# Where and on which engine the gate part of layer 2's modulation vector is computed

## The chip, the core and the metric

The kernel runs on one core of one Trainium2 chip. The core has five engines, each with its own in-order queue of instructions: TensorE (PE in the profile: matmuls, with PEld for the loading of the stationary operand), VectorE (DVE), ScalarE (ACT), GpSimd (POOL) and SyncE (SP, which here only issues DMA transfers). The engines wait for one another with semaphores. The metric is the device time of one execution in microseconds (us); lower is better.

## The reference

Two layers are applied to 256 latent tokens x (sample A, s = 0) and 256 context tokens (sample B, s = 1), each 2048 wide. Both layers start from a modulation vector that depends on a conditioning vector alone, one for the latent tokens and one for the context:

```
def adaln_params(cond, w_mod, b_mod):
    return jnp.split(jax.nn.silu(cond) @ w_mod + b_mod, 3, axis=-1)   # shift, scale, gate

def modulate(x, gain, shift, scale):
    return rmsnorm(x, gain) * (1 + scale) + shift

def deltanet_layer(x, ctx, c, c_ctx, ..., update_ctx):               # layer 2
    sh, sc, gt = adaln_params(c, w_mod, b_mod)
    sh_c, sc_c, gt_c = adaln_params(c_ctx, w_mod, b_mod)
    ...
    x = x + gt[:, None] * deltanet_out(o_xf + flip_t(o_xb), zx, o_norm, w_out)
    if update_ctx:                                                   # not in the last layer
        ctx = ctx + gt_c * deltanet_out(o_cf + flip_t(o_cb), zc, o_norm, w_out)
```

`w_mod` is 2048 x 6144 in float32. Shift and scale of layer 2 are used for both samples, at the start of the layer. Its gate is used for sample A alone, and only at the layer's very end. Layer 1 has neighbourhood attention (8 heads, "NA"), latent attention (8 heads, "MLA") and an output product; layer 2 is a gated DeltaNet; a final norm follows.

## The kernel before

Every dense product is made in float32 precision out of three products of halves: a weight block is loaded as `raw` (four buffers, DMA at L71), its high part `whi` is taken by ScalarE (L77) and the rest `wlo` by VectorE (L78), and TensorE makes hi by hi (L90), hi by lo (L91) and lo by hi (L92). One `unit` is a 128-column block of outputs for all 512 tokens: two weight halves of 8 x 3 matmuls each. A scheduler puts the instructions of each engine in order from the program's order, the buffers and an estimate of its own of when each is ready; the queue of each engine then runs in that order. A transfer waits in SP's queue for its buffer, and all that stand behind it wait too.

The modulation vector of a layer, `mods[l]`, has 48 blocks of 128, made in 12 chunks of 512 columns: chunks 0 to 3 are the shift, 4 to 7 the scale, 8 to 11 the gate. A chunk needs the 2048 x 512 float32 block of `w_mod`, which comes in eight transfers of 512 KB into `mraw`. There are two ways to make a chunk:

- `adaln` (L107), on TensorE: the conditioning is the stationary operand (32 columns wide, four row groups side by side), the weights are streamed through into the PSUM tile `pmod` (L127). VectorE copies it to `macc` (L133), TensorE transposes it (L136, `pmt`), and VectorE adds up the row groups and the bias (L138, L139). Both samples cost no more than one.
- `adaln_lanes` (L147), on VectorE: for each of 16 slices of 128 weight rows and each sample, one instruction adds slice times conditioning to `lacc` (L161 for the first slice, L163 for the others): 32 instructions on 128x512 elements for a chunk. They are called lane steps below. Then TensorE adds up the partitions with a matmul against ones (L170, `pml`), and VectorE adds the bias (L173). `lacc` and `pml` have one buffer each.

Both are generators. `later` (L307) strings them together, and each weight half of a `unit` (L316) advances the one in `ahead` by `pace` steps, so that the pieces lie between the pieces of other work in the program's order.

The program goes through layer 1 in these stages, with the chunks of layer 2 that each of them holds:

- the NA heads (seven of them one after another, each with its units of q, k, v and gate). `ahead` holds layer 1's own chunks 8 to 11 and layer 2's chunks 0 and 1, all as lane steps, with `pace` 1;
- units and rope for MLA, then the eighth NA head. From here `ahead` holds chunks 2, 3 and 8 of layer 2 as `adaln`, in a pool `mr2`, with three buffers for `mraw`;
- the eight MLA heads (L348, L381, L372 to L388 are attention's instructions), one step of `ahead` each; after them chunk 9 as `adaln` (L473), and the split of the gated heads into `gh`, `gl` (L480, L481);
- the output product: 16 units with the weights `ab_wo`, each followed by `x1A` and `x1B` (L493). Here chunks 4 to 7 stand as lane steps, begun after the first of these units;
- the modulate of layer 2 (L221 to L229, into `hh` and `hl`), while the first two units of layer 2 already consume it block by block. Chunks 10 and 11 stand here as `adaln` (L499, L504);
- then layer 2 (its first units are U_BA, whose output ScalarE takes at L635 and L636, and the K unit).

The gate of layer 2 is read by `project` (L606 to L611) near the end of the kernel, at `mods[1][:, 32 + u, 0:1]`: sample 0 only.

Of the kernel before, what the change touches and what calls it, by code (L numbers as in the profile page):

```python
# [8 lines left out]
F32 = mybir.dt.float32  # L9
F32R = mybir.dt.float32r  # L10
AF = mybir.ActivationFunctionType
ALU = mybir.AluOpType
# [14 lines left out]
def trunk_kernel(ctx: ExitStack, tc: tile.TileContext, g):  # L27
    nc = tc.nc
    V, A, PE, P = nc.vector, nc.scalar, nc.tensor, nc.gpsimd
# [14 lines left out]
    def cst(name, shape, src=None):  # L44
        t = const.tile(shape, F32, name=name, tag=name)
        if src is not None:
            nc.scalar.dma_start(t, src)
        return t
# [16 lines left out]
    mods = [cst(f"mod{l}", [128, 48, 2]) for l in range(2)]  # L65
# [80 lines left out]

    def adaln_lanes(l, ps, pm, tp, chunks, after=None):  # L147

        wm, bmod, gain = ((g["ab_wm"], ab_bmod, ab_gain), (g["dn_wm"], dn_bmod, dn_gain))[l]
        for ch in chunks:  # L150
            acc = tp.tile([128, 2, 512], F32, name="lacc", tag="lacc", bufs=1)
            for kg in range(4):
                for i in range(2):
                    raw = tp.tile([128, 2, 512], F32, name="mraw", tag="mraw", bufs=3)
                    with tc.issue_after(after) if after else nullcontext():
                        nc.sync.dma_start(raw, wm[ch, kg].rearrange("p (q c) -> p q c", q=4)[:, 2 * i:2 * i + 2])
                    for q in range(2):
                        k = 4 * kg + 2 * i + q
                        for s in range(2):
                            if k == 0:  # L160
                                V.tensor_scalar(acc[:, s], raw[:, q], cond[:, k, s:s + 1], None, op0=ALU.mult)  # L161
                            else:
                                V.scalar_tensor_tensor(acc[:, s], raw[:, q], cond[:, k, s:s + 1], acc[:, s],  # L163
                                                       op0=ALU.mult, op1=ALU.add)
                    if i == 0 or kg < 3:
                        yield
            pt = ps.tile([128, 4, 2], F32, name="pml", tag=pm, bufs=1)
            for j in range(4):
                for s in range(2):
                    PE.matmul(pt[:, j, s:s + 1], acc[:, s, j * 128:j * 128 + 128], ones[:, 0:1], start=True, stop=True)  # L170
            f = slice(4 * ch, 4 * ch + 4)
            md = mods[l][:, f]
            V.tensor_tensor(md, pt, bmod[:, f].unsqueeze(2).broadcast_to([128, 4, 2]), op=ALU.add)  # L173
            if 4 <= ch < 8:
                f = slice(4 * ch - 16, 4 * ch - 12)
                V.tensor_scalar(Am[l][:, f], md, 1.0, None, op0=ALU.add)
                V.tensor_tensor(Am[l][:, f], Am[l][:, f], gain[:, f].unsqueeze(2).broadcast_to([128, 4, 2]), op=ALU.mult)
            yield

    def steps(it, n=1000):  # L180
        for _ in range(n):
            if next(it, it) is it:
                break
# [18 lines left out]
    def blocks_of(*tiles, n=T):  # L202
        return [[t[:, c:c + 128] for t in tiles] for c in range(0, n, 128)]
# [39 lines left out]
    with tc.tile_pool(name="s0", bufs=2) as tp, tc.tile_pool(name="s0p", bufs=1, space=PSUM) as ps:  # L243
# [26 lines left out]
        def mods_of(j):  # L270
            k0, n = GROUPS[j]
            return adaln(0, ps, ("pmod", "aux"), tp, [(k0, n), (16 + k0, n)], bufs=MB)
# [8 lines left out]
        for j, (k0, n) in enumerate(GROUPS):  # L281
            ahead = mods_of(j + 1) if j < end else iter(())
# [19 lines left out]
    with tc.tile_pool(name="ab", bufs=2, reuse_waits="tile") as tp, \  # L302
            tc.tile_pool(name="abp", bufs=2, space=PSUM, reuse_waits="tile") as ps:
        u, last_mm = NS, None
        mr = tc.alloc_tile_pool(name="mr", bufs=2)

        def later(pool, parts, after=None):  # L307
            for l, chunks, lanes in parts:
                if lanes:
                    yield from adaln_lanes(l, ps, "pm", pool, chunks, after)  # L310
                else:
                    yield from adaln(l, ps, ("pm", "pm"), pool, [(4 * ch, 4) for ch in chunks], after=after)

        ahead, pace = later(mr, ((0, range(8, 12), 1), (1, (0, 1), 1))), 1

        def unit(xh, xl, src=None):  # L316
            nonlocal u, last_mm
# [126 lines left out]
        ch = big.tile([128, KT, T], F32R, name="ch", tag="hh")  # L444
# [6 lines left out]
                V.tensor_tensor(ch[:, 8 + j], craw[:, j], ch[:, j].bitcast(F32), op=ALU.subtract)  # L451
        cr.release()
        mr = tc.alloc_tile_pool(name="mr2", bufs=2, reuse_waits="tile")
        ahead = later(mr, ((1, (2, 3, 8), 0),))
        attend(*na7)
        w = load_split(g["ab_wqr"])
        for j in range(4):
# [3 lines left out]
        for h in range(8):  # L461
            w = load_split(g["ab_wb"][h], 1536)
            o = []
            for j, (k0, name, sc) in enumerate(((0, "qT", MLA_SCALE), (4, "kT", 1.0), (4, "vT", 1.0))):
                p = mm_tile()
                last_mm = dense(p, w, j * 512, 4, ch, ch[:, 8:], k0)
# [3 lines left out]
            attend(*o, 8 + h, None, ([qr[r, 4 * i + h // 2] for i in range(2)], [kr[r, i] for i in range(2)]))  # L470

        steps(ahead)
        steps(later(mr, ((1, (9,), 0),), last_mm))  # L473
        pace = 0
        gh = big.tile([128, KT, T], F32R, name="gh", tag="hh")
        gl = big.tile([128, KT, T], F32R, name="gl", tag="hl")
# [7 lines left out]
        for j in range(KT):  # L484
# [4 lines left out]
            if j == 0:  # L489
                ahead, pace = later(mr, ((1, (4, 5, 6, 7), 1),), last_mm), 1  # L490
# [5 lines left out]
            if j % 4 == 3:  # L496
                nc.sync.dma_start(x1d[:, j - 3:j + 1], x1[0][:, j - 3:j + 1])
        steps(ahead)
        ahead = later(mr, ((1, (10, 11), 0),), last_mm)  # L499
        rb = rstd_bcast(blocks_of(qacc, sq), 4, D, ps, "st", tp)  # L500
        hh = big.tile([128, KT, T], F32R, name="hh", tag="hh")
        hl = big.tile([128, KT, T], F32R, name="hl", tag="hl")
        modulate(1, lambda k, s: x1[s][:, k], rb, hh, hl, tp)
        steps(ahead)  # L504
        mr.release()

    abx.release()
# [106 lines left out]
    with tc.tile_pool(name="dn", bufs=2, reuse_waits="tile") as tp, \  # L614
# [10 lines left out]
        ch = tp.tile([128, 1792], F32, name="cumh", tag="sp", bufs=1)[:, :1152].rearrange("p (a n) -> p a n", a=9)  # L625
# [752 lines left out]
```

## Time and profile before

| | |
|---|---|
| Median of three runs | 2572.16 us (2571.8 to 2573.67) |
| The profiled execution's own time | 2568.78 us |
| Span of its trace | 2567.0 us |
| TensorE busy | 2464.1 us (96%), 16586 matmuls |
| VectorE busy | 1849.9 us (72%), 3543 instructions |
| ScalarE busy | 1126.9 us (44%) |
| GpSimd busy | 271.2 us (11%) |
| Moved by DMA | 394.3 MB, 154 GB/s in the mean |

The stages that the change touches lie in the trace as follows: the seven NA heads from 278 to 574 us, the units and rope up to 690, the eighth NA head and the first MLA products up to 746, the eight MLA heads and the split of `gh`, `gl` to 911, the output product to 1072, and the modulate with the first units of layer 2 to 1122. All times are from the span's start. In the rows of the profile, "L163 DVE" is line 163 of the kernel on VectorE; "x4" is four instructions in a row, and the number after the start is the time from the start of the first to the end of the last; "[1.67 <-DVE x1B L493]" says that the engine was idle for 1.67 us before, and what released it.

### The profile page before, as it was taken

What the parts mean: (1) busy time and instruction counts of PE and PEld (TensorE: products, weight loads), DVE (VectorE), ACT (ScalarE), POOL (GpSimd) and SP (SyncE); (2) the same over time, 40 slices, a digit from 0 to 9 for tenths busy, and PEclk for the clock granted to TensorE, in tenths of its full rate; (3) what the DMA queues carried; (4) which work ended last, traced back from release to release, by engine and by line L of the source; (5) the groups of instructions that cost most, each with busy time, mean ns of one, the idle gap of its engine ahead of it and who ended that gap; (6) DMA issues with size and microseconds to landing.
All of it is one profiled execution on the core that took longest, in us unless ns stands there. A gap on an engine that the chain in (4) does not pass through costs nothing.

```text
span 2567.0 us, 43390 instructions
## 1 busy us (share of the span) xinstructions
PE 2464.1 (96%) x16586; PEld 2004.8 (78%) x16586; DVE 1849.9 (72%) x3543; ACT 1126.9 (44%) x2452; POOL 271.2 (11%) x261
## 2 busy tenths in 40 slices
PE   6999999999999999989899999999999999999998
PEld 4657888888767778768888888887777777778898
DVE  4544788873455688758999999997677777777654
ACT  4223323332334422377556555643444545445453
POOL 0000000000000000123222222300000000003000
PEclk9999999999999999999999999998999999999999
DMA  8872655532343366644444545573333333335454
GB/s 253 292 253 87 201 169 166 179 123 90 105 157 113 106 216 226 221 141 145 159 154 149 153 154 168 151 226 96 87 105 114 117 98 107 112 91 181 150 189 138
DMA packets 201809, 394.30 MB, mean 154 GB/s; under 512 B 68224, under 2 KB 109696, under 8 KB 201472
## 3 DMA queue, kind: packets, MB, share of 16 engines
q1 hardware_dynamic: 200448, 389.98, 48.4%
q8 instruction: 131, 2.15, 0.3%
q10 hardware_dynamic: 1152, 1.54, 0.2%
q14 instruction: 78, 0.64, 0.1%
HBM read 356.28 MB, written 35.13 MB: 152 GB/s over the span
## 4 chain that ended last, share of the span: by engine, by line
PE 75%; DVE 12%; issue 6%; DMA 3%; ACT 3%; SPq 0%; POOL 0%; DVEq 0%; POOLq 0%; ACTq 0%
PE mm L90 19%; PE mm L91 17%; PE mm L92 17%; PE pks L983 3%; PE pmod L127 3%; DVE wlo L78 3%; PE sp L348 2%; PE ptr L995 2%; DVE acc L561 2%; DVE outer L768 1%; PE po L348 1%; DVE X L770 1%; DVE U L776 1%; PE ptr L1028 1%; DMA mraw<-dn_wm 1%
## 5 line engine op out<-in xcount | busy, mean ns | idle before, releaser
L90 PE MATMUL mm<-hh,whi 128*128 128x512 f32 (+1 forms) x2784 | 987.8, 355 | 2.9 <-ACT t L636 2.4
L92 PE MATMUL mm<-hh,wlo 128*128 128x512 f32 (+1 forms) x2784 | 962.1, 346 | 8.4 <-DVE wlo L78 7.8
L91 PE MATMUL mm<-hl,whi 128*128 128x512 f32 (+1 forms) x2784 | 960.7, 345 | 0.5 <-issue 0.5
L77 ACT CAST whi<-raw 128x1024 fp32r<-128x1024 f32 (+2 forms) x346 | 338.3, 979 | 674.7 <-PE mm L91 541.0
L90 PEld LDWEIGHTS mm<-hh,whi 128*128 128x128 f32 x2784 | 534.1, 192 | 112.5 <-issue 32.7
L92 PEld LDWEIGHTS mm<-hh,wlo 128*128 128x128 f32 x2784 | 534.3, 192 | 73.9 <-DVE wlo L78 9.2
L91 PEld LDWEIGHTS mm<-hl,whi 128*128 128x128 f32 x2784 | 534.8, 192 | 62.9 <-issue 7.5
L78 DVE TENSOR_TENSOR wlo<-raw,whi 128x1024 fp32r<-128x1024 f32 (+2 forms) x346 | 401.8, 1163 | 210.5 <-ACT whi L77 209.1
L163 DVE SCALAR_TENSOR_TENSOR lacc<-mraw,cond,lacc 128x512 f32<-128x512 f32 x300 | 208.2, 743 | 0.0
L561 DVE SCALAR_TENSOR_TENSOR acc<-cin,taps,acc 128x508 f32<-128x508 f32 (+3 forms) x256 | 194.6, 761 | 6.6 <-ACT acc L552 4.3
L1005 DVE SCALAR_TENSOR_TENSOR vl<-ptr,egm,vh 128x128 fp32r<-128x128 f32 x224 | 64.6, 346 | 99.2 <-ACT rf L1002 39.4
L711 POOL TENSOR_TENSOR rhs<-ghl,incl 128x512 fp32r<-128x512 f32 (+1 forms) x96 | 110.1, 1163 | 193.7 <-PE pd L713 174.3
L768 DVE SCALAR_TENSOR_TENSOR outer<-L,bv,X 128x31 f32<-128x31 f32 (+15 forms) x248 | 118.2, 476 | 5.2
L127 PE MATMUL pmod<-mraw,cond 128*32 128x512 f32 (+2 forms) x640 | 94.9, 505 | 24.1 <-DMA mraw<-ab_wm 18.6
L1089 DVE TENSOR_TENSOR wlo<-raw,whi 128x1024 fp32r<-128x1024 f32 x84 | 102.5, 1220 | 14.3 <-ACT whi L1081 14.2
L194 POOL TENSOR_TENSOR rs<-ms,half 128x4 f32<-128x4 f32 (+1 forms) x5 | 4.7, 950 | 986.1 <-DVE ms L192 986.1
L770 DVE TENSOR_TENSOR X<-X,outer 128x31 f32<-128x31 f32 (+15 forms) x248 | 99.4, 401 | 4.7
L90 PE MATMUL mm<-gh,whi 128*128 128x512 f32 x256 | 100.7, 395 | 1.7 <-DVE x1B L493 1.7
L91 PE MATMUL mm<-gl,whi 128*128 128x512 f32 x256 | 100.5, 393 | 0.2 <-DVE gl L481 0.2
L92 PE MATMUL mm<-gh,wlo 128*128 128x512 f32 x256 | 100.1, 391 | 0.0
L575 ACT ACTIVATE ac<-acc 128x128 f32<-128x128 f32 x160 | 37.4, 300 | 141.0 <-DVE acc L561 141.0
L999 ACT ACTIVATE vh<-ptr,egm 128x128 fp32r<-128x128 f32 x224 | 71.2, 375 | 61.2 <-PE ptr L995 59.1
(289 smaller groups left out, 3550.4 us busy)
## 6 DMA issues: line engine op xcount, KB each, us to landing
raw<-dn_w SPq DMA_DIRECT2D x194, 512.0 KB, 4.1
mraw<-dn_wm SPq DMA_DIRECT2D x96, 512.0 KB, 4.6
mraw<-ab_wm SPq DMA_DIRECT2D x88, 512.0 KB, 5.5
raw<-ab_w SPq DMA_DIRECT2D x66, 512.0 KB, 3.8
raw<-dn_wo SPq DMA_DIRECT2D x64, 512.0 KB, 3.7
raw<-ab_wo SPq DMA_DIRECT2D x32, 512.0 KB, 4.7
raw<-ab_w SPq DMA_DIRECT2D x32, 256.0 KB, 3.6
spt<-sp SPq DMA_DIRECT2D x64, 128.0 KB, 2.5
```

The lines of the kernel that those rows point to most:

```text
L77: A.copy(hi[:, :m], raw[:, :m])
L78: V.tensor_tensor(lo[:, :m], raw[:, :m], hi[:, :m].bitcast(F32), op=ALU.subtract)
L90: PE.matmul(ps, wh[:, c], xh[:, k0 + k, sl], start=first and k == 0, stop=False)
L91: PE.matmul(ps, wh[:, c], xl[:, k0 + k, sl], start=False, stop=False)
L92: end = PE.matmul(ps, wl[:, c], xh[:, k0 + k, sl], start=False, stop=last and k == kt - 1)
L127: PE.matmul(pmod[32 * q:32 * q + 32, :m], cond[:, 4 * kg + q, :], raw[c // 1024][:, half + c % 1024:half + c % 1024 + m], start=kg == 0, s ...
L163: V.scalar_tensor_tensor(acc[:, s], raw[:, q], cond[:, k, s:s + 1], acc[:, s], op0=ALU.mult, op1=ALU.add)
L561: V.scalar_tensor_tensor(o3[:, :, i0:i1], p3[:, :, i0 + d:i1 + d], taps[:, ch, t:t + 1], o3[:, :, i0:i1], op0=ALU.mult, op1=ALU.add)
L711: P.tensor_tensor(rhs, ghl[i].bitcast(F32)[:, d, kh * 8:kh * 8 + 2 * n].unsqueeze(2).broadcast_to(sh), incl[:, c].unsqueeze(1).broadcast_t ...
L768: V.scalar_tensor_tensor(o, L[:, rows, k:k + 1].broadcast_to([128, n, m]), bv[:, k:k + 1], X[:, k:k + 1, cols].broadcast_to([128, n, m]), ...
L770: V.tensor_tensor(X[:, rows, cols], X[:, rows, cols], o, op=ALU.subtract)
L1089: V.tensor_tensor(w, raws[j], h.bitcast(F32), op=ALU.subtract)
```

## The change

The lane steps get a case with one sample: for the gate chunks of layer 2 (8 to 11) `adaln_lanes` now makes 16 lane steps instead of 32, and half of the `pml` matmuls. These four chunks are appended to the list of the NA heads, behind chunks 0 and 1, and `pace` there is 2 instead of 1. Chunk 8 is taken out of the MLA heads' list, chunk 9 from behind it, and chunks 10 and 11 from the modulate.

```diff
--- before.py
+++ after.py
@@ -146,8 +146,10 @@
 
     def adaln_lanes(l, ps, pm, tp, chunks, after=None):
 
+
         wm, bmod, gain = ((g["ab_wm"], ab_bmod, ab_gain), (g["dn_wm"], dn_bmod, dn_gain))[l]
         for ch in chunks:
+            ns = 1 if l == 1 and ch >= 8 else 2
             acc = tp.tile([128, 2, 512], F32, name="lacc", tag="lacc", bufs=1)
             for kg in range(4):
                 for i in range(2):
@@ -156,7 +158,7 @@
                         nc.sync.dma_start(raw, wm[ch, kg].rearrange("p (q c) -> p q c", q=4)[:, 2 * i:2 * i + 2])
                     for q in range(2):
                         k = 4 * kg + 2 * i + q
-                        for s in range(2):
+                        for s in range(ns):
                             if k == 0:
                                 V.tensor_scalar(acc[:, s], raw[:, q], cond[:, k, s:s + 1], None, op0=ALU.mult)
                             else:
@@ -164,13 +166,13 @@
                                                        op0=ALU.mult, op1=ALU.add)
                     if i == 0 or kg < 3:
                         yield
-            pt = ps.tile([128, 4, 2], F32, name="pml", tag=pm, bufs=1)
+            pt = ps.tile([128, 4, ns], F32, name="pml", tag=pm, bufs=1)
             for j in range(4):
-                for s in range(2):
+                for s in range(ns):
                     PE.matmul(pt[:, j, s:s + 1], acc[:, s, j * 128:j * 128 + 128], ones[:, 0:1], start=True, stop=True)
             f = slice(4 * ch, 4 * ch + 4)
-            md = mods[l][:, f]
-            V.tensor_tensor(md, pt, bmod[:, f].unsqueeze(2).broadcast_to([128, 4, 2]), op=ALU.add)
+            md = mods[l][:, f, :ns]
+            V.tensor_tensor(md, pt, bmod[:, f].unsqueeze(2).broadcast_to([128, 4, ns]), op=ALU.add)
             if 4 <= ch < 8:
                 f = slice(4 * ch - 16, 4 * ch - 12)
                 V.tensor_scalar(Am[l][:, f], md, 1.0, None, op0=ALU.add)
@@ -311,7 +313,7 @@
                 else:
                     yield from adaln(l, ps, ("pm", "pm"), pool, [(4 * ch, 4) for ch in chunks], after=after)
 
-        ahead, pace = later(mr, ((0, range(8, 12), 1), (1, (0, 1), 1))), 1
+        ahead, pace = later(mr, ((0, range(8, 12), 1), (1, (0, 1), 1), (1, range(8, 12), 1))), 2
 
         def unit(xh, xl, src=None):
             nonlocal u, last_mm
@@ -451,7 +453,7 @@
                 V.tensor_tensor(ch[:, 8 + j], craw[:, j], ch[:, j].bitcast(F32), op=ALU.subtract)
         cr.release()
         mr = tc.alloc_tile_pool(name="mr2", bufs=2, reuse_waits="tile")
-        ahead = later(mr, ((1, (2, 3, 8), 0),))
+        ahead = later(mr, ((1, (2, 3), 0),))
         attend(*na7)
         w = load_split(g["ab_wqr"])
         for j in range(4):
@@ -470,7 +472,6 @@
             attend(*o, 8 + h, None, ([qr[r, 4 * i + h // 2] for i in range(2)], [kr[r, i] for i in range(2)]))
 
         steps(ahead)
-        steps(later(mr, ((1, (9,), 0),), last_mm))
         pace = 0
         gh = big.tile([128, KT, T], F32R, name="gh", tag="hh")
         gl = big.tile([128, KT, T], F32R, name="gl", tag="hl")
@@ -496,12 +497,10 @@
             if j % 4 == 3:
                 nc.sync.dma_start(x1d[:, j - 3:j + 1], x1[0][:, j - 3:j + 1])
         steps(ahead)
-        ahead = later(mr, ((1, (10, 11), 0),), last_mm)
         rb = rstd_bcast(blocks_of(qacc, sq), 4, D, ps, "st", tp)
         hh = big.tile([128, KT, T], F32R, name="hh", tag="hh")
         hl = big.tile([128, KT, T], F32R, name="hl", tag="hl")
         modulate(1, lambda k, s: x1[s][:, k], rb, hh, hl, tp)
-        steps(ahead)
         mr.release()
 
     abx.release()
```

Lines of the changed kernel are two higher than before from the lane steps on, and one lower from the output product on.

VectorE in an MLA head. Before, with one copy of a gate chunk out of PSUM (`macc`) among the attention's instructions (`PT`, `rc`, `pr`, `mx`, `goA`) and the weights' low halves (`wlo`):

```order
L78 TENSOR_TENSOR wlo<-raw,whi 128x512
L341 TENSOR_TENSOR kT<-mm,kT 128x512
L133 COPY macc<-pmod 128x512
L341 TENSOR_TENSOR PT<-pt,PT 128x4x128
L377 RECIPROCAL rc<-sm 128x1
L378 TENSOR_SCALAR pr<-pr,rc 128x256
L78 TENSOR_TENSOR wlo<-raw,whi 128x1024
L372 TENSOR_REDUCE mx<-sp 128x1
L377 RECIPROCAL rc<-sm 128x1
L378 TENSOR_SCALAR pr<-pr,rc 128x512
L388 TENSOR_TENSOR goA<-po,goA 128x256
```

The changed kernel, at the same place:

```order
L343 TENSOR_TENSOR PT<-pt,PT 128x4x128
L379 RECIPROCAL rc<-sm 128x1
L165 SCALAR_TENSOR_TENSOR lacc<-mraw,cond,lacc 128x512 x2
L380 TENSOR_SCALAR pr<-pr,rc 128x256
L78 TENSOR_TENSOR wlo<-raw,whi 128x1024
L374 TENSOR_REDUCE mx<-sp 128x1
L165 SCALAR_TENSOR_TENSOR lacc<-mraw,cond,lacc 128x512 x2
L343 TENSOR_TENSOR PT<-pt,PT 128x4x128
L165 SCALAR_TENSOR_TENSOR lacc<-mraw,cond,lacc 128x512
L379 RECIPROCAL rc<-sm 128x1
L165 SCALAR_TENSOR_TENSOR lacc<-mraw,cond,lacc 128x512 x2
L380 TENSOR_SCALAR pr<-pr,rc 128x256
```

The lane steps here (L165, which was L163) are those of chunks 4 to 7, which the diff doesn't touch: in the program they still stand behind the first unit of the output product, but the buffers of `mr2` are no longer used by chunks 8 and 9 ahead of them, and the scheduler puts them in between the attention's instructions. Between the tenth `qT` of the kernel and the first `x1A` there are now 114 lane steps (before: 16), and in the output product 14 (before: 112). In the NA heads, between the first lane step and the eighth `qT`, there are 256 (before: 192).

VectorE in the modulate. Before:

```order
L221 SCALAR_TENSOR_TENSOR mh<-x1A,Am_86,rb 128x256
L221 SCALAR_TENSOR_TENSOR mh<-x1B,Am_86,rb 128x256
L224 SCALAR_TENSOR_TENSOR hl<-mh,mod_84,hh 128x256
L133 COPY macc<-pmod 128x512
L221 SCALAR_TENSOR_TENSOR mh<-x1A,Am_86,rb 128x256
L221 SCALAR_TENSOR_TENSOR mh<-x1B,Am_86,rb 128x256
L221 SCALAR_TENSOR_TENSOR mh<-x1A,Am_86,rb 128x256
L221 SCALAR_TENSOR_TENSOR mh<-x1B,Am_86,rb 128x256
L138 TENSOR_REDUCE mod_84<-pmt 128x8
L139 TENSOR_TENSOR mod_84<-mod_84,vecs 128x8
L221 SCALAR_TENSOR_TENSOR mh<-x1A,Am_86,rb 128x256
L221 SCALAR_TENSOR_TENSOR mh<-x1B,Am_86,rb 128x256
```

The changed kernel:

```order
L226 SCALAR_TENSOR_TENSOR hl<-mh,mod_84,hh 128x256
L223 SCALAR_TENSOR_TENSOR mh<-x1A,Am_86,rb 128x256
L223 SCALAR_TENSOR_TENSOR mh<-x1B,Am_86,rb 128x256
L226 SCALAR_TENSOR_TENSOR hl<-mh,mod_84,hh 128x256
L223 SCALAR_TENSOR_TENSOR mh<-x1A,Am_86,rb 128x256
L223 SCALAR_TENSOR_TENSOR mh<-x1B,Am_86,rb 128x256
L223 SCALAR_TENSOR_TENSOR mh<-x1A,Am_86,rb 128x256
L223 SCALAR_TENSOR_TENSOR mh<-x1B,Am_86,rb 128x256
L226 SCALAR_TENSOR_TENSOR hl<-mh,mod_84,hh 128x256
```

The copies of `pmod` and the sums of `pmt` are gone from the modulate; the same holds for the second chunk, whose copy stood behind the modulate's last `mh` before.

SP's queue, from the end of the output product into layer 2. Before:

```order
L122 DMA mraw<-dn_wm 128x1024
L497 DMA x1d<-x1A 128x1024
L71 DMA raw<-dn_w 128x1024
L122 DMA mraw<-dn_wm 128x1024 x11
L71 DMA raw<-dn_w 128x1024
L122 DMA mraw<-dn_wm 128x1024
L71 DMA raw<-dn_w 128x1024
L122 DMA mraw<-dn_wm 128x1024
L518 DMA incl<-dnc 128x192
L518 DMA taps<-taps 128x320
L518 DMA ad<-ad 128x2
L626 DMA cumh<-dnc 128x1152
L71 DMA raw<-dn_w 128x1024 x4
```

The changed kernel:

```order
L71 DMA raw<-dn_w 128x1024 x4
L498 DMA x1d<-x1A 128x1024
L71 DMA raw<-dn_w 128x1024 x3
L517 DMA incl<-dnc 128x192
L517 DMA taps<-taps 128x320
L517 DMA ad<-ad 128x2
L625 DMA cumh<-dnc 128x1152
L71 DMA raw<-dn_w 128x1024 x4
```

The sixteen transfers of chunks 10 and 11 stood among the first weights of layer 2 and ahead of its constants (`incl`, `taps`, `ad`, `cumh`); now the weights and the constants follow the output product's own transfers at once. The 32 transfers of the four chunks stand in the NA heads' part of this queue instead.

## The prediction

> **What bounds the kernel now.** I read the page's engine shares first, then the chain of waits, then the stages that the change touches.
>
> ```profile
> span 2567.0 us, 43390 instructions
> PE 2464.1 (96%) x16586; PEld 2004.8 (78%) x16586; DVE 1849.9 (72%) x3543; ACT 1126.9 (44%) x2452; POOL 271.2 (11%) x261
> PE 75%; DVE 12%; issue 6%; DMA 3%; ACT 3%; SPq 0%; POOL 0%; DVEq 0%; POOLq 0%; ACTq 0%
> ```
>
> TensorE is busy for 96% of the span and makes up 75% of the chain, so work taken from TensorE should shorten the kernel wherever nothing else ends last. VectorE's 72% is a mean, though. By stage (busy time of each engine, number of instructions, granted clock, DMA share, GB/s):
>
> ```profile
> core 0: us, PE busy (x) PEld busy (x) DVE busy (x) ACT busy (x) POOL busy (x), PEclk, DMA share, GB/s
> 278.00:574.00 296.00, 296.00 (x1487) 250.26 (x1486) 241.26 (x405) 92.61 (x162) 0.00 (x0) 1.00 0.52 169
> 746.00:911.00 165.00, 162.44 (x840) 118.98 (x839) 102.54 (x227) 69.58 (x166) 0.00 (x0) 1.00 0.36 118
> 911.00:1072.00 161.00, 159.89 (x725) 133.27 (x726) 128.56 (x196) 39.36 (x59) 0.00 (x0) 0.99 0.68 219
> 1072.00:1122.00 50.00, 44.95 (x207) 25.35 (x207) 31.29 (x64) 30.67 (x66) 18.42 (x16) 0.93 0.64 206
> ```
>
> The rows are the seven NA heads, the MLA heads, the output product and the modulate. In the first three TensorE leaves nearly no gap; in the modulate it has gaps and waits for others. The lane steps alone (the same windows, instructions that touch `lacc`; the columns are PE, PEld, DVE):
>
> ```profile
> 278.00:574.00 296.00, 11.32 (x96) 12.05 (x96) 130.07 (x192) 1.00 0.52 169
> 746.00:911.00 165.00, 0.00 (x0) 0.00 (x0) 10.41 (x16) 1.00 0.36 118
> 911.00:1072.00 161.00, 5.85 (x51) 6.18 (x52) 75.74 (x113) 0.99 0.68 219
> ```
>
> One lane step costs VectorE 75.74/113 = 0.67 us.
>
> **The change, part by part.**
>
> *NA heads.* 64 lane steps (16 for each of four chunks) come in: 64 x 0.67 = 43 us. Of these the order has 15 behind the seventh head, where they are 10 us, so VectorE's load here goes from 241.3 to about 274 us of 296, 93%. That it can run so without TensorE stalling is shown by 50 us of the same stage:
>
> ```profile
> 300.00:350.00 50.00, 50.00 (x251) 42.26 (x250) 46.26 (x80) 17.75 (x31) 0.00 (x0) 1.00 0.61 203
> ```
>
> There VectorE was busy for 46.26 of 50 us, and TensorE for all 50. What TensorE does get is the `pml` matmuls: 11.32 us for the six chunks of two samples, 1.89 each, so half of that for one sample, and 4 x 0.94 = +3.8 us. `lacc` has one buffer: the next chunk's first lane step waits for TensorE's `pml`, and `pml` for the last lane step; with ten chunks in place of six I add 1 us (0 to 4). The 32 transfers of 512 KB are 16.8 MB in 296 us, 57 GB/s more, 226 in the mean, which is little above the 219 of the output product, where TensorE was busy for 159.89 of 161 us. I take nothing for them.
>
> *MLA heads.* Chunks 8 and 9 leave TensorE:
>
> ```profile
> L127 PE MATMUL pmod<-mraw,cond 128*32 128x512 f32 x72 | 13.1, 603 | 1.1 <-DMA mraw<-dn_wm 1.1
> L136 PE MATMUL pmt<-ident,macc 128*128 128x128 f32 x12 | 1.9, 277 | 0.0
> ```
>
> Of the 72 records 64 are theirs (the rest is chunk 3's), of the 12 transposes 8: 11.6 + 1.1 + 1.3 = 14.0 us. But the order shows a second effect: chunks 4 to 7 of the output product move up into this stage, 114 lane steps in place of 16, and three of their four `pml` groups with them, 3 x 1.89 = 5.7 us of TensorE. TensorE then needs 165 - 14.0 + 5.7 = 157 us. VectorE needs 102.54 - 10.41 + 114 x 0.67 - 1.4 (two `macc` copies at 0.7, a row below) = 167 us. So VectorE takes the stage over, and the 14 us that TensorE saves are not had. A loaded VectorE has been seen at the end of this very stage, where lane steps stood ahead of `x1A`:
>
> ```profile
> 882.84:911.10 28.26, 26.74 (x130) 21.66 (x130) 28.03 (x66) 6.34 (x14) 0.00 (x0) 1.00 0.46 152
> 909.11 2.07 DVE L163 SCALAR_TENSOR_TENSOR lacc<-mraw,cond,lacc 128x512 f32<-128x512 f32 x3
> 911.10 0.47 DVE L493 SCALAR_TENSOR_TENSOR x1A<-mm,mod,xr 128x256 f32<-128x256 f32 x1
> 912.11 0.76 PE L90 MATMUL mm<-gh,whi 128*128 128x512 f32 x1 [1.67 <-DVE x1B L493]
> 912.10:915.50 3.40, 3.39 (x8) 2.72 (x9) 3.40 (x6) 1.10 (x3) 0.00 (x0) 0.50 0.83 265
> ```
>
> For 28 us it was 99% busy; TensorE, two units ahead by then, waited 1.67 us for `x1B`, and then ran 3.4 us at a granted clock of 0.50. With attention's chains in the queue (scores, maximum, exponential, reciprocal, product, transpose) I take a share between the 99% here and the 92.5% of the NA row, nearer the first because here VectorE is the one that others wait for: 97%, 167/0.97 = 172 us, +7 (bounds: TensorE's 157, -8, if the lane steps slip out of the stage; 167/0.88 = 190, +25, at a share well under any loaded stretch shown).
>
> By the Trainium skill, "TensorE: Matmul & The Clock Gate" ("HAM oscillation" and "A second HAM failure mode: psum-queue depth-cycling"), a TensorE that is fed in bursts can swing between full and half clock, even by frequent small idle times. The trace shows one such window above, 3.4 us long after a 1.67 us gap, and none after a gap of 1.1 us; what the rule would make of this stage is the third rival.
>
> *Output product.* The three `pml` groups leave it, -5.7 us on a full TensorE. Its VectorE load halves, which brings nothing.
>
> *Modulate.* Chunks 10 and 11 leave it. VectorE stands in order behind the copies of `pmod`, and SP behind the transfers:
>
> ```profile
> 1071.73 0.48 DVE L493 SCALAR_TENSOR_TENSOR x1A<-mm,mod,xr 128x256 f32<-128x256 f32 x1 [1.83 <-PE mm L92]
> 1076.23 27.16 SPq L122 DMA_DIRECT2D mraw<-dn_wm x11
> 1077.84 1.87 PE L199 MATMUL rb<-dg,ones 128*128 128x128 f32 x8
> 1080.26 0.91 ACT L222 ACTIVATE hh<-mh,mod 128x256 fp32r<-128x256 f32 x2 [7.05 <-DVE mh L221]
> 1092.92 0.69 DVE L133 COPY macc<-pmod 128x512 f32<-128x512 f32 x1 [3.35 <-PE pmod L127]
> 1094.03 0.91 ACT L222 ACTIVATE hh<-mh,mod 128x256 fp32r<-128x256 f32 x2 [3.37 <-DVE mh L221]
> 1110.92 1.31 POOL L229 TENSOR_TENSOR hl<-mh,hh 128x512 fp32r<-128x512 f32 x1 [2.49 <-ACT mh L227]
> 1116.23 1.99 ACT L77 CAST whi<-raw 128x1024 fp32r<-128x1024 f32 x2 [5.39 <-PE mm L91]
> 1117.92 0.69 DVE L133 COPY macc<-pmod 128x512 f32<-128x512 f32 x1 [8.43 <-PE pmod L127]
> 1118.24 1.28 ACT L635 ACT_TABLE_LOAD   x1
> 1120.99 0.68 ACT L636 ACTIVATE t<-mm,ad 64x512 f32<-64x512 f32 x1 [0.39 <-DMA ad<-ad]
> 1121.72 0.39 PE L90 MATMUL mm<-hh,whi 128*128 128x256 f32 x1 [2.40 <-ACT t L636]
> L222 ACT ACTIVATE hh<-mh,mod 128x256 fp32r<-128x256 f32 x32 | 14.7, 497 | 13.5 <-DVE mh L221 13.4
> L227 ACT ACTIVATE mh<-mh,mod 128x256 f32<-128x256 f32 x22 | 10.5, 493 | 0.0
> L127 PE MATMUL pmod<-mraw,cond 128*32 128x512 f32 x64 | 15.1, 693 | 1.9 <-DMA mraw<-dn_wm 1.9
> ```
>
> What ends this stage is the third unit's first matmul at 1121.72, and its chain reads backwards: `t`, the table load, `whi`, the last matmul of the first two units, the last `hl`. After the change: `rb` starts some 0.7 us earlier (the `pmod` block ahead of it is gone). ScalarE then has 32 + 22 activations, 0.40 us from start to start, and two `whi` of 1 us each, 23.6 us from 1079.6, and about 1 us of small gaps (its 6.4 us of idle time within the stage, 13.4 less the 7.05 at the start, without the 3.37 behind `macc` and the 2.1 behind VectorE late in it): 1104.2. The last `hl` takes 1.3, to 1105.5; TensorE no longer has 15.1 us of `pmod` between, and ends some eight matmuls later, 1.8 us: 1107.3. Then `whi` 1.0, the table 1.3, two activations 1.2, and the third unit starts at about 1110.8, for 1121.72: -10.9 us. Bounds: -4 if only the first `macc` wait and `rb`'s delay go (the `pmod` then were only fillers), and -14.5 if ScalarE ran with no gap and the table were loaded early.
>
> **The sum**: +3.8 + 1 (NA) + 7 (MLA) - 5.7 (output product) - 10.9 (modulate) = -4.8 us against the profiled execution's 2568.78, which lies 3.4 us under the median of the runs shown; against the median 2572.2 - 4.8 = 2567.4, say 2567. This kernel's measurement tells a difference of about 0.2% (5.1 us) from none, so the likeliest case lies at the edge of what is told as faster.
>
> **The rivals.**
>
> 1. *Slower: VectorE's queue in the MLA heads runs with holes.* In order, each `mx`, `rc` and `pr` that is waited for behind one or two lane steps delays ScalarE and TensorE, and the holes in turn VectorE. At 88% the stage is 190 us, +25, and the NA heads lose 3 more: 25 + 4.8 + 3 - 5.7 - 10.9 = +16.2, 2588. It decides from 165 + 11.8 = 177 us (a share of 94%) on, where the gains of the other stages are used up. For it: before, VectorE waits within the MLA heads in the middle of its chains, 62 us of 165 idle. Against it: 99% at the stage's end, and lane steps that are ready fill such holes.
>
> 2. *The TensorE view*: VectorE hides all. Then MLA gives -8, and the sum is 3.8 - 8 - 5.7 - 10.9 = -20.8: 2551. For it: 75% of the chain is TensorE. Against it: VectorE's 167 us, unless the lane steps slip into the output product, where VectorE's load falls from 128.6 us by 99 lane steps to 62 of 161.
>
> 3. *Clock.* If the 172 - 157 = 15 us of TensorE's idle time in the MLA heads fall as gaps like the 1.67 us one, nine of them each bring 3.4 us at half clock, 1.7 us lost: TensorE needs 157 + 15, and with part of the gaps left the stage takes some 181 us, +16: 2576. This is what the Trainium skill's rule named above would make of it. Against it: the gap of 1.1 us in these heads left the clock at 1.00, as the stage's row has it, and VectorE's share may keep single gaps shorter than that.
>
> 4. *The modulate gives only half*, because ScalarE and the table loads keep the third unit late: -5 in place of -10.9, 2573, no change.
>
> **How the numbers follow.** Likeliest case 0.42, own range 2557 to 2575 (the MLA term from 0 to +13, the modulate by 3 to either side); rival 1 0.22; rival 2 0.12; rival 3 0.08; rival 4 0.16. Faster by over 0.2% (under 2567.0): half of the likeliest, all of rival 2, a little of 4: 0.22 + 0.12 + 0.04 = 0.38. Slower (over 2577.3): most of rival 1, half of 3, the edges of the likeliest and 4: 0.20 + 0.04 + 0.05, 0.29. The rest, 0.33, is no change. The range goes from the edge of rival 2, 2552, to just under rival 1's 2588, at 2586, and leaves out about half of each.
>
> **What would show it.** Right: in the MLA heads VectorE busy above 95% with some 114 lane steps and TensorE at about 157 us of some 172; no `macc` in the modulate, the third unit's first matmul about 38 to 40 us after the last `x1A` (before: 1121.72 - 1071.73 = 50); NA heads about 5 us longer with TensorE full. Wrong: TensorE waits for VectorE in the NA heads; a granted clock under 1.00 in the MLA heads; an MLA stage of 160 us (rival 2) or over 177 (rival 1); a third unit that still starts 45 us after `x1A`.

## The result: 0.9% slower, and where the time went in the profile after

The changed kernel takes 2595.29 us (median of four runs, 2591.34 to 2600.29) against 2572.91 for the kernel before: 1.009 times as long, 95% interval 1.007 to 1.011. The prediction was 2567, range 2552 to 2586, with a chance of 0.29 on slower: outside the range, and on the other side of no change. Of the four runs two lie near 2591.5 us, the traced one (2591.7) among them, and two near 2599.6; e2 below leaves out one run of ten, of 9184 us.

The page of the changed kernel shows the same busy engines. Its clock row (tenths of full speed in 40 equal slices of the span) has new dents; the last row is that of the kernel before:

```profile
span 2589.9 us, 43243 instructions
PE 2456.0 (95%) x16474; PEld 2016.6 (78%) x16474; DVE 1887.3 (73%) x3599; ACT 1129.2 (44%) x2450; POOL 273.5 (11%) x261
PEclk9999999998999989989999999999999999999999
PEclk9999999999999999999999999998999999999999
```

TensorE is busy for 8 us less than before and the span is 22.9 us longer, so most of the time lies in gaps. Marks that both programs have (the last instruction of the eighth NA head, the first and last `x1A`, the first `rb` of layer 2, the third unit's first matmul) give the stages in us, from both traces (differences are taken before rounding):

| from, to | before | after | difference | predicted |
|---|---|---|---|---|
| start to the seventh NA head's end | 573.2 | 573.9 | +0.7 | +4.8 |
| to the eighth NA head's end (units and rope between) | 137.9 | 165.1 | +27.2 | 0 |
| to the first `x1A` (MLA heads) | 199.9 | 212.3 | +12.4 | +7 |
| to the last `x1A` (output product) | 160.6 | 153.7 | -7.0 | -5.7 |
| to `rb` and the third unit (modulate) | 50.0 | 40.1 | -9.9 | -10.9 |
| to the end | 1445.3 | 1444.9 | -0.4 | 0 |

In the first row the changed kernel's execution is helped by its start: its first lane step comes 1.9 us earlier (275.7 in place of 277.5 us). From there on the heads take 298.2 us in place of 295.7, +2.5; only two of the four new `pml` groups lie in them.

The stages of the changed kernel by window (columns as before: PE, PEld, DVE, ACT, POOL, granted clock, DMA share, GB/s; the rows from 739 to 951 are the MLA heads as a whole, their beginning and two stretches of their middle; the last two are the output product and the modulate):

```profile
278.00:574.00 296.00, 296.00 (x1496) 250.41 (x1494) 269.06 (x450) 91.74 (x158) 0.00 (x0) 1.00 0.65 209
574.00:598.00 24.00, 3.35 (x18) 3.05 (x18) 14.48 (x21) 1.96 (x3) 0.00 (x0) 0.61 0.59 206
739.00:951.30 212.30, 196.51 (x966) 148.30 (x962) 176.10 (x362) 82.10 (x187) 0.00 (x0) 0.96 0.44 141
739.00:781.00 42.00, 38.91 (x191) 24.77 (x187) 19.86 (x40) 15.23 (x28) 0.00 (x0) 1.00 0.51 168
790.00:870.00 80.00, 76.03 (x397) 59.11 (x395) 73.61 (x151) 31.23 (x70) 0.00 (x0) 1.00 0.44 139
870.00:930.00 60.00, 53.53 (x251) 42.59 (x252) 56.30 (x125) 27.57 (x73) 0.00 (x0) 0.86 0.37 118
951.00:1105.00 154.00, 152.71 (x676) 126.54 (x676) 66.14 (x89) 39.41 (x60) 0.00 (x0) 1.00 0.44 140
1105.00:1145.00 40.00, 31.55 (x135) 24.85 (x134) 27.90 (x57) 29.25 (x64) 18.34 (x16) 0.83 0.24 76
```

Up to 574 us VectorE is 91% busy and TensorE loses nothing, as predicted. Then come 24 us in which TensorE works for 3.35. The timeline there, TensorE, VectorE and ScalarE:

```profile
573.77 0.39 PE L92 MATMUL mm<-hh,wlo 128*128 128x512 f32 x1
575.36 1.05 PE L172 MATMUL pml<-ones,lacc 128*128 128x1 f32 x8 [1.20 <-DVE lacc L165]
595.14 1.84 PE L172 MATMUL pml<-ones,lacc 128*128 128x1 f32 x8 [18.73 <-DVE lacc L165]
597.70 0.80 PE L90 MATMUL mm<-hh,whi 128*128 128x512 f32 x1 [0.72 <-ACT craw L419]
...
578.07 0.48 DVE L163 TENSOR_SCALAR lacc<-mraw,cond 128x512 f32<-128x512 f32 x1 [1.46 <-DMA mraw<-dn_wm]
578.59 3.90 DVE L165 SCALAR_TENSOR_TENSOR lacc<-mraw,cond,lacc 128x512 f32<-128x512 f32 x5
593.46 1.54 DVE L165 SCALAR_TENSOR_TENSOR lacc<-mraw,cond,lacc 128x512 f32<-128x512 f32 x2 [1.46 <-DMA mraw<-dn_wm]
...
597.06 1.08 ACT L419 COPY craw<-mm 128x512 f32<-128x512 f32 x2 [22.04 <-PE pml L172]
```

Read it from the last row back. ScalarE's copy into `craw` has waited 22 us, for a `pml` matmul; that one waited 18.73 us for VectorE's last lane step of chunk 11; VectorE only began this chunk at 578.07, when the heads were over. `craw` stands in the pool `cr`, which takes the room of the pool `mr` with `lacc` and `mraw`: it can't be written before the last lane step's sum has been read. The first two units after the heads were already multiplied and hold both of their PSUM buffers until `craw` takes them, so TensorE has nothing else. In the kernel before, the same copy waits for the same matmul too, but for 1.5 us:

```profile
ACT craw L417 <- PE pml L170: 1.5, 1, 1.5
```

TensorE's rows say it as well: between the last product of the heads (573.77 us) and the first one behind `craw` (597.70) it has the two `pml` groups of chunks 10 and 11 and nothing else. That `craw` waits because of the room is read from the program and from this wait; no run gave `craw` a room of its own.

The gaps of 1.20, 18.73 and 0.72 us make 20.7 of the 27.2. After them TensorE runs at half clock until about 603 us, which costs another 3, and the two `pml` groups (1.05 and 1.84 us) have no other work beside them.

In the MLA heads VectorE is 92 and 94% busy in the two stretches from 790 on, and TensorE is no longer full. What TensorE waited for there (engine, line, releaser: us in total, times, longest), changed kernel:

```profile
PE sp L350 <- ACT pr L377: 6.5, 8, 1.2
PE po L350 <- ACT PT L342: 3.7, 3, 2.9
PE pmod L127 <- DMA mraw<-dn_wm: 2.3, 2, 1.5
```

The first is new, and the second was 0.7 us before. In both TensorE waits for ScalarE: for an exponential (`pr`) and for a copy of the transposed product (`PT`). The obvious reading, that the exponential waits for a maximum (`mx`) that stands behind lane steps on VectorE, isn't what the trace shows. ScalarE waits less for maxima than before (changed kernel, then the kernel before):

```profile
ACT pr L377 <- DVE mx L374: 11.2, 5, 5.9
ACT pr L375 <- DVE mx L372: 19.4, 11, 3.6
```

In the six longest of the eight waits for `pr` the exponential follows directly behind a copy of `PT` on ScalarE, and its maximum had been ready for 0.7 us or more. For the longest wait of TensorE, 2.91 us at 907.72 us, `PT` stands behind thirteen copies into `gh`, from 903.10 to 907.19 us. So TensorE is held up by the order of ScalarE's queue here; how the lane steps bring that about, and which link of the attention's chain is late first, stays open.

Last, the modulate: no `macc` any more, and the third unit's first matmul 40.1 us after the last `x1A`:

```profile
1110.17 2.04 PE L201 MATMUL rb<-dg,ones 128*128 128x128 f32 x8 [1.81 <-DVE dg L200]
1137.64 0.91 ACT L224 ACTIVATE hh<-mh,mod 128x256 fp32r<-128x256 f32 x2 [2.08 <-DVE mh L223]
1142.40 1.28 ACT L634 ACT_TABLE_LOAD   x1
1145.03 0.38 PE L90 MATMUL mm<-hh,whi 128*128 128x256 f32 x1 [3.05 <-ACT t L635]
```

### The profile page after: what moved, and what is told of

Its sections match the earlier page's. It is cut to its first block, busy times and chain, and to the rows that moved or that the text cites. A ratio compares the mean times of both kernels' runs of the same rounds, so it can differ in the third digit from the quotient of the medians.

```text
span 2589.9 us, 43243 instructions
## 1 busy us (share of the span) xinstructions
PE 2456.0 (95%) x16474; PEld 2016.6 (78%) x16474; DVE 1887.3 (73%) x3599; ACT 1129.2 (44%) x2450; POOL 273.5 (11%) x261
## 4 chain that ended last, share of the span: by engine, by line
PE 75%; DVE 10%; issue 6%; ACT 4%; DMA 3%; POOL 1%; SPq 0%; DVEq 0%; POOLq 0%; ACTq 0%
PE mm L90 19%; PE mm L91 18%; PE mm L92 18%; PE pks L982 3%; PE ptr L994 2%; PE sp L350 2%; PE pmod L127 2%; DVE wlo L78 2%; DVE acc L560 2%; DMA mraw<-dn_wm 2%; PE po L350 1%; PE ptr L1027 1%; DVE U L775 1%; PE psu L1013 1%; DVE outer L767 1%
## 5 line engine op out<-in xcount | busy, mean ns | idle before, releaser
L165 DVE SCALAR_TENSOR_TENSOR lacc<-mraw,cond,lacc 128x512 f32<-128x512 f32 x360 | 255.6, 741 | 8.5 <-DMA mraw<-dn_wm 7.4
L294 DVE TENSOR_TENSOR zs<-zs,mm 128x512 f32<-128x512 f32 x72 | 49.2, 686 | 65.5 <-PE mm L92 65.3
```

## The experiments

The theory after the result: three effects that add up, (a) the chain of lane steps doesn't fit into the NA heads, and `craw` waits for its end; (b) 114 lane steps among the MLA heads' instructions load VectorE, and TensorE pays; (c) the modulate's gain is real. Rivals: the NA stage suffers from VectorE's load or the transfers as a whole; the MLA heads suffer from the loss of chunks 8 and 9 as fillers of TensorE.

**e1: two gate chunks fewer.** Chunks 10 and 11 are not computed (zeros stand in their place).

```diff
-ahead, pace = later(mr, (..., (1, (0, 1), 1), (1, range(8, 12), 1))), 2
+V.memset(mods[1][:, 40:48, 0:1], 0.0)
+ahead, pace = later(mr, (..., (1, (0, 1), 1), (1, (8, 9), 1))), 2
```

> The changed kernel, with gate chunks 10 and 11 left out (their part of the modulation vector is set to zero, so half of the gate is not computed); everything else as changed. Theory (the chain of lane steps is too long for the NA heads: the buffers of the lane steps have to be given up to the next stage's craw, and TensorE waits for the last pml): with two gate chunks fewer the chain ends before the NA heads do, TensorE has no gap of 19 us at 575 us, the eighth NA head's end comes back from 739 to about 713 us, and the time falls by 24 to 28 us, to 2569 (2566 to 2573). The MLA heads stay slow (212 us from the eighth NA head's end to the first x1A). Rival (VectorE's load of 91% and the added transfers slow the NA stage as a whole): half of the excess stays, 2582 or more, and gaps are spread over the heads.

Measured 2564.97 us, 0.9978 (0.9969 to 0.9988) of before. The time from the seventh to the eighth head's end is 141.6 us, in place of 165.1; the MLA heads stay slow at 215.4. It is 30 us faster than the changed kernel by the medians, and 28 when each is compared with the kernel before as it was measured beside it, the upper end of what was expected. The traced execution, 2570.12 us, is the longest of the ten. `craw` waits for no `pml` any more. (a) holds, and its rival, a load spread over the stage, doesn't.

**e2: chunks 4 to 7 held back.** The first lane step of each of them is ordered on VectorE behind the last `gl`.

```diff
+                last_gl = V.tensor_tensor(gl[:, k, sl], ...).ins
...
-                ahead, pace = later(mr, ((1, (4, 5, 6, 7), 1),), last_mm), 1
+                ahead, pace = later(mr, ((1, (4, 5, 6, 7), 1),), last_mm, last_gl), 1
...
+                                with tc.issue_after(hold) if hold else nullcontext():
                                     V.tensor_scalar(acc[:, s], raw[:, q], ...)
```

> The changed kernel, with the first lane step of each chunk 4 to 7 ordered on VectorE behind the last split of gl, so that these chunks stay in the output product. Theory (the MLA heads are slow because VectorE holds 114 lane steps among attention's instructions): the stretch from the eighth NA head's end to the first x1A falls from 212 to about 187 us (before: 200, less 14 us of chunks 8 and 9), the granted clock there goes back to 1.00, the output product goes back from 154 to 160 us, and the sum is 2595 - 25 + 6 = 2576 (2572 to 2581). The gap at the end of the NA heads stays. Rival (the MLA heads are slow because chunks 8 and 9 no longer fill TensorE's gaps, so that its clock falls, whatever VectorE does): the stretch stays above 205 us at a clock under 0.98, 2595 or above.

Measured 2575.72 us, 1.0017 (1.0008 to 1.0027) of before. The MLA stretch is 189.7 us, the output product 159.1. Its MLA rows (the same middle as above, then the whole stretch):

```profile
790.00:870.00 80.00, 80.00 (x419) 62.91 (x419) 47.99 (x104) 35.16 (x82) 0.00 (x0) 1.00 0.16 50
739.70:929.40 189.70, 182.79 (x918) 137.23 (x914) 111.40 (x244) 79.94 (x186) 0.00 (x0) 0.99 0.25 82
```

TensorE is full where the changed kernel left 4 of 80 us, and of its waits for `pr` one is left (the changed kernel had eight, 6.5 us):

```profile
PE sp L351 <- ACT pr L378: 1.4, 1, 1.4
```

(b) holds in that the lane steps among the attention's instructions cost the time: without them TensorE is full in the middle of the stage, and chunks 8 and 9 aren't needed to fill it. The edge moves the chunks' transfers out of the stage too (50 GB/s in place of 139); but the waits that went were for ScalarE, and none for a transfer of theirs.

**e3: both causes taken away.** As e2, with chunks 10 and 11 as one-sample lane steps in the MLA heads; the whole vector is computed.

```diff
-        ahead, pace = later(mr, ((0, range(8, 12), 1), (1, (0, 1), 1), (1, range(8, 12), 1))), 2
+        ahead, pace = later(mr, ((0, range(8, 12), 1), (1, (0, 1), 1), (1, (8, 9), 1))), 2
...
-        ahead = later(mr, ((1, (2, 3), 0),))
+        ahead = later(mr, ((1, (2, 3), 0), (1, (10, 11), 1)))
```

> The changed kernel, with chunks 4 to 7 held back to the output product as in e2, and gate chunks 10 and 11 taken out of the NA heads and put as one-sample lane steps into the MLA heads behind chunks 2 and 3 (32 lane steps there in place of 114). Theory (both causes add up): no gap at the NA heads' end (-26), MLA stretch about 188 us (-24), output product +6, the modulate as in the changed kernel: 2595 - 44 = 2551 (2546 to 2558), faster than before by 0.8%. Rival (lane steps in the MLA heads cost TensorE whatever their number): MLA stretch near 200, 2563 or above.

Measured 2553.57 us (2553.01 to 2556.41), 0.9929 (0.9913 to 0.9946) of before: the fastest version, and 1.6% under the changed kernel. The MLA stretch is 195.6 us, more than the 188 expected and 5.9 more than in e2, where no lane step stands ahead of the last `gl`:

```profile
713.90:909.50 195.60, 188.00 (x934) 141.21 (x930) 130.08 (x279) 81.27 (x187) 0.00 (x0) 0.97 0.37 123
```

TensorE's idle time in this row is 7.6 us (195.60 - 188.00), in e2's row 6.9. So 32 lane steps hardly made TensorE wait, at a VectorE share of two thirds (130 of 196 us). The 5.9 us are the `pml` groups of the two chunks, 2.1 us, and the clock: 10.2 us at half clock in place of 3.4, which costs 3.4 more. The expectation had left both out. Whether the lane steps brought on the half clock isn't shown.

**e4: the modulate alone.** The kernel before, with only chunks 10 and 11 moved. Against the changed kernel:

```diff
-        ahead, pace = later(mr, ((0, range(8, 12), 1), (1, (0, 1), 1), (1, range(8, 12), 1))), 2
+        ahead, pace = later(mr, ((0, range(8, 12), 1), (1, (0, 1), 1), (1, (10, 11), 1))), 2
...
-        ahead = later(mr, ((1, (2, 3), 0),))
+        ahead = later(mr, ((1, (2, 3, 8), 0),))
...
         steps(ahead)
+        steps(later(mr, ((1, (9,), 0),), last_mm))
```

> The kernel before, with only chunks 10 and 11 moved out of the modulate, into the NA heads as one-sample lane steps with pace 2; chunks 8 and 9 stay as TensorE products in the MLA heads, and the order then leaves chunks 4 to 7 in the output product. Theory (the modulate's gain of 10.5 us stands by itself, the NA heads bear two gate chunks without a gap): 2573 - 10.5 + 0 to 2 = 2563 (2560 to 2566); MLA stretch 200 us and clock as before. Rival (part of the modulate's gain in the changed kernel came from the output product's empty VectorE): 2568 or above.

Measured 2561.67 us, 0.9961 (0.9947 to 0.9976) of before. From the last `x1A` to the third unit it takes 40.1 us, as in the changed kernel, though the output product's VectorE is as loaded as before. (c) holds: 9.9 us, by itself.

**e5: two samples again.** The changed kernel with 32 lane steps for a gate chunk, with the same transfers.

```diff
-            ns = 1 if l == 1 and ch >= 8 else 2
+            ns = 2
```

> The changed kernel with the case of one sample undone: the gate chunks make 32 lane steps each again, with the same transfers. Theory (in the gap at the end of the NA heads TensorE waits for a chain of lane steps on VectorE): 64 more lane steps lengthen the chain; nearly all of them fall behind the heads, at 0.74 us each, so the gap of 19 us grows by about 45 us and the time goes to about 2640 (2630 to 2655). Rival (the gap is set by the transfers of the weights, 512 KB each, whose number doesn't change): the gap stays within 5 us of what it was, 2595 to 2600.

One run: 2628.65 us, before 2571.66. `craw` waits 56.4 us:

```profile
ACT craw L419 <- PE pml L172: 56.4, 1, 56.4
PE pml L172 <- DVE lacc L165: 45.9, 3, 20.4
```

TensorE's wait grows by 26 us (45.9 against 19.9), not by 45, and not by nothing. In the gap a chunk of 32 steps takes 20.8 us from its first lane step to its last, one of 16 steps 17: with two samples VectorE paces it (0.65 us a step), with one the transfers do, eight of 512 KB in 17 us. Halving the steps bought little there, but over the whole chain it is worth 34 us: with two samples the last lane step ends at 629.4 us, with one at 595.0. Both theories were too simple.

**e6: a second `lacc`.** The room of a third `mraw` goes to it.

```diff
-            acc = tp.tile([128, 2, 512], ..., tag="lacc", bufs=1)
+            acc = tp.tile([128, 2, 512], ..., tag="lacc", bufs=2 if na else 1)
...
-                    raw = tp.tile([128, 2, 512], ..., tag="mraw", bufs=3)
+                    raw = tp.tile([128, 2, 512], ..., tag="mraw", bufs=2 if na else 3)
```

> The changed kernel, with two buffers for lacc and two in place of three for mraw in the NA heads (the room is the same). Theory (the chain of chunks is long because each chunk's first lane step waits until TensorE has read the chunk before out of the one lacc buffer, 5 to 7 us between chunks, nine times): the chain ends 15 to 40 us earlier, the gap of 19 us falls under 8, and the time goes to about 2575 (2568 to 2583). Rival (VectorE's load or the transfers set the chain's length, and two buffers for transfers make it worse): the gap stays at 19 us or grows, 2595 or above.

Measured 2602.66 us, 1.0118 (1.0101 to 1.0135) of before: a miss. The pauses between chunks are gone (a two-sample chunk takes 35.7 us from start to start, in the changed kernel 38.8), and chunk 8 begins 17 us earlier (491.2 in place of 508.4), but the lane steps now wait for transfers within the chunks, with attention's instructions queued behind them. A one-sample chunk takes 28 to 30 us from start to start, where it took 21 to 25, so the gain is lost again, and the heads themselves end 17.5 us later (591.4 against 573.9). VectorE's waits for transfers (in total, times, longest):

```profile
DVE lacc L166 <- DMA mraw<-dn_wm: 31.8, 20, 3.7
```

Its row of the heads' window: TensorE idle for 5 us, and VectorE less busy than in the changed kernel:

```profile
278.00:574.00 296.00, 291.09 (x1446) 243.33 (x1446) 264.22 (x445) 88.84 (x154) 0.00 (x0) 0.99 0.63 207
```

**e9: e6 with one `lacc` again**, so two `mraw` buffers alone.

```diff
-            acc = tp.tile([128, 2, 512], ..., tag="lacc", bufs=2 if na else 1)
+            acc = tp.tile([128, 2, 512], ..., tag="lacc", bufs=1)
```

> e6 with the second lacc buffer taken away again: the changed kernel with two buffers for mraw in place of three in the NA heads, and one for lacc. It parts e6's two changes. Theory A (the second lacc buffer shortens the chain of chunks by the 5 to 7 us between chunks, and e6 lost more than that by its smaller number of transfer buffers): without it the chain ends 25 to 50 us later than e6's 602 us, and the time is 2625 to 2650. Theory B (the number of lacc buffers doesn't matter; VectorE's order and the transfers pace the chain): the same as e6 within 6 us, 2597 to 2609.

Measured 2615.28 us, 1.0173 (1.0156 to 1.019) of before; the chain ends at 613.0 us (e6: 602.2, the changed kernel: 595.0). Neither theory's range was met. In time, the second `lacc` is worth 13 us (against e6) and the third `mraw` 20 (against the changed kernel): both set the chain's length. The third `mraw` counts in the one-sample chunks alone: chunk 8 begins at 509.9 us, nearly as in the changed kernel, and the 18 us by which the chain ends later come after that. What the chain would take with both buffers wasn't tried.

**e8: three gate chunks in the NA heads**, the fourth in the MLA heads. Against e3:

```diff
-(1, (8, 9), 1)
+(1, (8, 9, 10), 1)
...
-(1, (10, 11), 1)
+(1, (11,), 1)
```

> e3 (chunks 4 to 7 held back) with three gate chunks in the NA heads (8, 9, 10) and one (11) as lane steps in the MLA heads. Theory (what counts is when the chain ends against the end of the heads): in the changed kernel chunk 10's pml came at 575.4 us, 1.2 us after TensorE had nothing else, so three chunks cost only 2 to 4 us at the end of the NA heads; 16 lane steps fewer in the MLA heads win 2 to 3; 2553 (2549 to 2558), the same as e3. Rival (each chunk in the NA heads costs in proportion, a quarter to a half of the 27 us): 2562 or above.

Measured 2561.52 us (2555.66 to 2563.36), 0.9954 (0.9939 to 0.9969) of before: 8 us slower than e3, where no difference was expected. The number lies next to the rival's 2562 and outside the theory's range. The trace shows the overrun that the theory had, and behind it 6.8 us at half clock (3.4 us lost) that it had not:

```profile
ACT craw L420 <- PE pml L173: 3.3, 1, 3.3
```

Counted from the first lane step, the eighth NA head ends 2.4 to 3.1 us later than before with two gate chunks (e1, e3, e4), 9.3 with three (e8), 29.7 with four (the changed kernel) and 63.0 with four of two samples (e5); `craw` waits for `pml` 0, 3.3, 22.0 and 56.4 us in them. So the cost isn't in proportion to the chunks: it is the wait, and 3 to 5 us more once there is one.

## Why the prediction was wrong, step by step

**NA heads: the step that failed.** The prediction wrote: "Of these the order has 15 behind the seventh head, where they are 10 us, so VectorE's load here goes from 241.3 to about 274 us of 296, 93%", and "I add 1 us (0 to 4)" for the chain through the one `lacc`. The load was right (269 us, 91%, TensorE full). But it took the lane steps behind the last head for a load that spills into a stage with room, asked only what VectorE can bear, and put the time between the seventh and the eighth head at nothing. They are the end of a chain with a deadline: `mr` is released there, and `craw` takes its room. The chain is longer than VectorE's load: ten chunks, each with pauses for `pml` and with other instructions of VectorE and transfers between its steps, from 275.7 to 595.0 us, when the heads end at 573.9. The cost was 27.2 us against 0 to 4. Without it the changed kernel would be near 2568; e1, with two chunks' work left out, is at 2565. None of the rivals had it: rival 1 named the right sign for another place, though the prediction's own signs of being wrong did name TensorE waiting for VectorE in the NA heads.

The trace before gave cause to ask: there a two-sample chunk took 29 to 36 us from its first lane step to its last, for 0.67 x 32 = 21 us of work. Six such chunks (190 us in sum) and four of half their mean length (63 us) make 253 us without any pause, and the shortest pause between two chunks was 11.7 us, nine times 105 us. That is an estimate, with a `pace` of 1; it doesn't give 319 us, but it shows that 296 weren't safe.

**MLA heads: the right sign, the wrong size, and a path that isn't the one described.** TensorE's saving is not had: +12.4 us against +7 (bounds -8 to +25), which carries the prediction's 165 us to 177, where its rival 1 begins. The share of 97% was nearly reached in the middle (92 to 94%), but the lane steps only begin at 781 us, behind chunk 3's copy at 777 us, so the stage's first 42 us passed at 47% (the row 739 to 781). Measured against e2, the 114 lane steps cost 22.6 us: 8.9 more idle time of TensorE, 6.6 from the clock (0.96 of 212 us against 0.99 of 190) and 5.7 of `pml` (three groups at 1.89); 1.4 us are not accounted for. Rival 3 has its clock here. Rival 1 has TensorE's idle time, but not by the late maxima it names: ScalarE waited less for them than before. What chunks 8 and 9 give back is 10.2 us (199.9 to 189.7), against 14.0.

**Output product**: -7.0 against -5.7. With the chunks back in it (e2) the stage takes 159.1 us, so their leaving is worth 5.4; the rest is the wait of 1.67 us for `x1B` and its half clock, which went in e2 too.

**Modulate: right.** -9.9 against -10.9, and alone (e4). No run parts the two causes that the prediction gave, the copies on VectorE and the transfers in SP's queue. The wait behind VectorE late in it stayed (2.08 us in the row above, 2.09 before), as did the wait for `t`.

**Range and chances.** The likeliest case had 0.42, and all its terms but one came within 6 us: the NA heads 4.1 below, the MLA heads 5.4 above, the output product 1.3 below, the modulate 1.0 above. These misses nearly cancel, which is luck: with the measured 27.2 us for the stage it had put at nothing, the sum would have been -4.8 + 27.2 = +22.4, and +22.4 was measured. The range ended at 2586, because the slower rival was priced only for the MLA heads.

## What to carry to other kernels

When background work moves into a stage, ask first by when it must be done, and who takes its buffers afterwards; then compare the length of its chain (pieces times the pace that the trace shows for a piece, pauses and transfers included) with the stage, not its busy time with the engine's spare time. While the chain ends in time it is nearly free; behind that, here, each microsecond of the wait counted in full, and 3 to 5 us more. And look at what the scheduler does with work that the diff doesn't touch: here the freed buffers let four other chunks move in among the attention's instructions, where they cost 22.6 us, and one ordering edge took that back. The same gate chunks in other places (e3) are 0.7% faster than before, where the change as made is 0.9% slower.

## What the runs showed of the hardware

The granted clock fell in steps of 3.4 us to 0.50, in all runs: 86.8 us in sum before, 145.4 in the changed kernel, 23.9 of them in and behind the gap at 574 us. In the MLA heads of the changed kernel gaps of 0.8 to 1.2 us at 795, 815, 836 and 853 us left the clock at 1.00 (the row 790 to 870 above), while 17 us at half clock followed from 873 us on, 6.8 of them around the gap of 2.91 us at 907 us. The Trainium skill, "TensorE: Matmul & The Clock Gate" ("A second HAM failure mode: psum-queue depth-cycling"), has frequent small idle times make the clock swing; here gaps of about a microsecond, one in 20 us, did not in the 80 us of that row. Whether they helped to bring on the stretch at 873 us stays open.

The prediction's third rival took a gap of 1.67 us to bring 3.4 us at half clock, and one of 1.1 us to bring none. The length of a gap alone doesn't decide it. In e1 a gap of 1.98 us was followed by 3.4 us at half clock, and in e2 one of 2.10 us, before the same matmuls, by none (each gap, then the clock in the window behind it):

```profile
727.46 1.06 PE L127 MATMUL pmod<-mraw,cond 128*32 128x512 f32 x2 [1.98 <-DMA mraw<-dn_wm]
727.50:730.90 3.40, 3.40 (x8) 1.47 (x9) 0.33 (x1) 0.00 (x0) 0.00 (x0) 0.50 0.81 265
754.05 1.05 PE L127 MATMUL pmod<-mraw,cond 128*32 128x512 f32 x4 [2.10 <-DMA mraw<-dn_wm]
754.00:760.00 6.00, 5.95 (x26) 4.29 (x27) 2.92 (x6) 1.73 (x3) 0.00 (x0) 1.00 0.68 231
```

The gap at 574 us cost more than its length, by the half clock behind it: some 3 us behind the gaps from 574 to 598 us. In the modulate of the changed kernel 13.7 us passed at half clock (0.83 in the row 1105 to 1145), where it was 6.8 before (0.93 from 1072 to 1122); with no `pmod` between the blocks of `hh`, TensorE is idle for 8.45 us of 40 there, before for 5.05 of 50.
